# A hybrid decoder step on one core: an earlier first step of the output projection, later gate products, and interleaved norm chains at the end

## The chip, the cores and the metric

The kernel runs on one core of one Trainium2 chip. Its time is the device time of one execution in microseconds (us); smaller is better. Times in the kernel's course are counted from the start of the profiled span.

## What is computed

One inference step of a one-layer decoder. A prompt of 1024 rows and 8 decode rows (1032 rows of width 2048) pass one input projection; an attention group with sparse top-k keys and an mLSTM group work on its parts; both results are multiplied by gates, sent through one output projection, added to the input and normalised.

```python
def merge(x, att_o, p, h_ml, ml_norm_w, w_out):
    B, T, _ = x.shape
    a = att_o.astype(x.dtype) * jax.nn.silu(p['az'])
    hn = h_ml * lax.rsqrt(jnp.mean(h_ml * h_ml, axis=-1, keepdims=True) + RMS_EPS)
    hn = hn * ml_norm_w.astype(jnp.float32).reshape(ML_HEADS, ML_V_DIM)
    mo = hn.reshape(B, T, ML_WIDTH).astype(x.dtype) * jax.nn.sigmoid(p['mo']) * jax.nn.silu(p['mz'])
    return x + jnp.concatenate([a, mo], axis=-1) @ w_out
...
    y_prompt = rmsnorm(xp, final_norm_w)
```

The change concerns only `merge`, its gates `az`, `mo`, `mz` (the last columns of the input projection), and the final `rmsnorm`.

## The kernel before

Every float32 operand of a matmul is split into a high part H and a low part L, and a product is three matmuls: H by H, H by L, L by H. The split of a 128x512 weight block is one cast on ACT (`wH`) and one subtraction on DVE (`wL`). Instructions of an engine run in the order in which they stand; `pin` and the `Ordered` wrappers (`oV`, `oS`, `oG`, `oY`, `oP`) keep hand-written parts in program order, and the rest is placed by a scheduler.

**The end of the input projection.** Gate columns are made by the loop over `seq` (L1890 on) with a Strassen-like scheme of seven products of 12 matmuls each, named by their operand: ..., S4, S3, A22. S3 and A22 of the last pair accumulate in the same PSUM bank `A_`: DVE must read `A_` after S3 (`out(v, 1, 2, A_, sv[1])`, L1758) before A22 goes on in it, and read it again after A22 (`out(v, 0, 2, A_, eng=V)`, L1760). Where another pair follows, its first product `w0` stands between S3 and A22; for the last pair there is none. What A22 gives becomes the last gate: ACT takes a tanh (L1823), DVE multiplies (L1824), and a DMA of the POOL queue stores it in `gateS` (L1825).

**The last 264 rows.** Rows 768 to 1031 go through the output projection first (`rest_step`, from `seq2`): a step is 12 matmuls of 128x264 with one weight block, already split by `cut_early` (steps one to six) or `cut2` (from step seven on). The other operand is made of "mixes", one per 128 features: a gate is loaded back from `gateS` (POOL queue, L1424), multiplied with the attention or mLSTM rows (`mx`, L1436 or L1438), and split into `mH` (ACT, L1441) and `mL` (DVE, L1442). The mixes numbered 6 and 7 are the last; they need the last gate. ACT's order has their two casts ahead of the weight cast of step seven (`wraw`).

**The first 768 rows.** Four turns c = 0 to 3 of seven products each (`prods`, j = 1 to 7: A11, A12, S1, S2, S4, S3, A22) give the rows in 6 blocks of 128 and 4 column groups of 512 (`yt[b][g]`). A product is 4 blocks k, each 9 matmuls of 128x512; while PE works on block k of one product, `cut3` splits block k of the next one, and `some(2)` runs two closures of the list `filler`. `begin()`, called after j = 3 of the first turn, loads attention rows (`mo`) and gates (`gx`) for the second half of the features and puts eight gate products (`one(n)`, on DVE) into `filler`.

**The end.** The last product (c = 3, j = 7) runs row block by row block. For each of the blocks b = 3, 4, 5: `evict` adds PSUM to `yt[b][1]` (DVE), `done` squares it with a row sum (ACT), `row_scale` makes the mean and the -0.5 power (two DVE operations, POOL), and `scale1`/`scale2` scale four tiles (two on ACT, two on DVE), each stored at once by SP (`put`). Column group 3 of these blocks was multiplied by the norm weight on POOL before. Blocks 0 to 2 are done the same way shortly ahead of that, as closures of `filler`.

Of the kernel before, what the change touches and what calls it, by code (L numbers as in the profile page):

```python
# [8 lines left out]
F32 = mybir.dt.float32  # L9
# [150 lines left out]
def body(tc, A, stop=None):  # L160
# [1729 lines left out]
    for v, (ph, n) in enumerate(seq):  # L1890
# [103 lines left out]
        product(w1, A_, "A22", False, True)
        with hi():
            out(v, 0, 2, A_, eng=V)
            if w0:
                seed(v + 1, A_, B_)
            if move:
                f2 = fill_load("A22", nx)  # L2000
                fill(f1)
                k = (turn[0] + 1) % 8
                free.extend(stage[k:] + stage[:k])
                for _ in range(4):
                    pfetch()
                fill(f2)
# [5 lines left out]
        now += 4  # L2012
    flush()

    korder = PRE
    oV, oS, oG, oY, oP = (Ordered(x, pin) for x in (V, SC, G, SY, PE))
    ready2 = ready + early_w
    ready.clear()
    c0, cn = CB[0]
    held = {}  # L2020

    def flat(x):
        return x.rearrange("p a b -> p (a b)")

    def split2(src, pool, bufs):
        H, L = [pool.tile([128, 4, 128], F32R, name="w" + x, bufs=bufs) for x in "HL"]
        oS.copy(H, src)
        oV.tensor_tensor(L, src, H.bitcast(F32), OP.subtract)
        return H, L

    def rest_step(t, q, H, L):
        if t not in held:
            held[t] = bank()[:, :cn]
        for k in range(4):
            mH, mL = mixb[0][korder[q * 4 + k]]
            for z, (w_, x_) in enumerate(((H, mH), (H, mL), (L, mH))):
                oP.matmul(held[t], w_[:, k, :], x_, start=(q + k + z == 0), stop=(q == 3 and k == 3 and z == 2))

    n1 = len(ready2)
    while mids and mids[0][1] not in PRE[12:]:  # L2040
        mixmake(*mids.pop(0))
    cut = {}

    def cut_early(j):
        cut[j] = split2(ready2[j], wst, 3)
# [235 lines left out]
    def row_scale(bs, last):
        b0, b1 = bs[0], bs[-1] + 1
        oV.tensor_scalar(ss[:, b0:b1, 5], ss[:, b0:b1, last], 1.0 / D, None, OP.mult)
        oV.tensor_tensor(ss[:, b0:b1, 5], ss[:, b0:b1, 5], ss[:, b0:b1, 4], OP.add)
        oG.tensor_tensor(ss[:, b0:b1, 6], ss[:, b0:b1, 5], mhalf.to_broadcast([128, b1 - b0]), OP.pow)

    def put(q, b, g):
        q.dma_start(A["yP"][b, :, g * 512:g * 512 + 512], yt[b][g])

    def scale1(b, last):  # L2290
        r, y = ss[:, b, 6:7], yt[b]
        u = min(g for g in range(4) if g != last)
        oS.activation(y[u], y[u], AF.Copy, scale=r)
        put(oY, b, u)
        oV.scalar_tensor_tensor(y[last], y[last], r, fw[last], OP.mult, OP.mult)
        put(oY, b, last)

    def scale2(b, last):
        r, y = ss[:, b, 6:7], yt[b]
        _, v, w = (g for g in range(4) if g != last)  # L2300
        oS.activation(y[v], y[v], AF.Copy, scale=r)
        put(oY, b, v)
        oV.tensor_scalar(y[w], y[w], r, None, OP.mult)
        put(oY, b, w)

    def done(bs, g):
        last = 3 if bs[0] < 3 else 1
        for b in bs:
            jk = pf[0].tile([128, 512], BF16, name="jk", bufs=2)
            oS.activation(jk, yt[b][g], AF.Square, accum_out=ss[:, b, g:g + 1])  # L2310
            if g != last:
                oG.tensor_tensor(yt[b][g], yt[b][g], fw[g], OP.mult)
        b0, b1 = bs[0], bs[-1] + 1
        if g == (1 if last == 3 else 3):
# [5 lines left out]
                oV.tensor_scalar(ss[:, b0:b1, 4], ss[:, b0:b1, 4], 1.0 / D, EPS, OP.mult, OP.add)  # L2320
            filler.append(sums)
        if g == last == 3:
            filler.extend((lambda: None, lambda: None, lambda: row_scale(bs, last), lambda: None, lambda: None))
            filler.extend(lambda b=b, f=f: f(b, last) for b in bs for f in (scale1, scale2))
        elif g == last:
            row_scale(bs, last)
            for b in bs:
                scale1(b, last)
                scale2(b, last)

    def gather1(b, g, p, sign):
        if (b, g) not in seen:
# [47 lines left out]
    def begin():  # L2380
# [105 lines left out]
    for p, d in enumerate(prods):  # L2486
        c, j = d["c"], d["j"]
        if p == len(prods) - 1:
            some(99)
            for b in range(3):  # L2490
                for k in range(4):
                    block(p, b, k, *cuts[p * 4 + k])
                evict(p, (b,))
                after(p, (b,))
            break
        for k in range(4):
            H, L = cuts.pop(p * 4 + k)
# [104 lines left out]
```

## Time and profile before

| | |
|---|---|
| median of 3 runs | 2017.35 us (2016.02 to 2018.61) |
| the profiled execution | 2015.65 us |
| its span in the profile | 2013.9 us |
| PE busy in the span | 1959.7 us |
| mean granted TensorE clock | 0.992 |

The profile is of one execution; 1.75 us of its time lie outside the span. A row of the timeline reads: start, duration, engine, line, operation, output and inputs, shapes, count, and in brackets the idle time of the engine before it with what ended it. L157 is the line of the `Ordered` helper, so that most instructions of the output projection bear it. Consecutive operations of DVE and ACT overlap by about 0.1 us, so that the distance of two starts is shorter than a duration.

### The profile page before, as it was taken

To read this page: it belongs to the slowest core of one execution; us is meant where nothing else is said; L and a number is where in the kernel's file an instruction comes from. 1 tells how busy PE (TensorE), PEld (TensorE's weight loads), DVE (VectorE), ACT (ScalarE), POOL (GpSimd) and SP (SyncE) were. 2 spreads that over 40 slices of the span, in tenths; PEclk is the share of its full clock that TensorE was granted. 3 is DMA by queue.
4 is the path that set the end of the run, shared out by engine and by line. 5 is a ranking of instruction groups with operands and counts; after the bars stand their busy time and mean duration, and the time that the engine had idled before them with its cause. 6 is when DMAs were issued, how large, how long until landed. Compare 5 with 4: busy or idle time off the path is not lost.

```text
span 2013.9 us, 35597 instructions
## 1 busy us (share of the span) xinstructions
PE 1959.7 (97%) x12404; PEld 1867.9 (93%) x12404; DVE 1310.4 (65%) x3115; ACT 1020.8 (51%) x2183; POOL 333.6 (17%) x442
## 2 busy tenths in 40 slices
PE   9999999999999999999999999989999999999997
PEld 8999999999999999998999999989999989978785
DVE  8574465446555563884667677677777677856766
ACT  8243246653343878313556565645555445535544
POOL 0000101100000000043000000132322230224472
PEclk9999999999999999999999999999999999999998
DMA  7686654532222222278456777499887868899994
GB/s 245 196 271 189 211 180 140 166 110 79 74 68 64 65 71 63 75 237 230 110 141 187 208 191 192 133 296 282 249 254 221 235 195 268 272 263 202 210 212 151
DMA packets 259821, 362.80 MB, mean 180 GB/s; under 512 B 39109, under 2 KB 156937, under 8 KB 259641
## 3 DMA queue, kind: packets, MB, share of 16 engines
q1 hardware_dynamic: 231945, 301.48, 48.3%
q0 software_dynamic: 27264, 58.87, 14.7%
q8 instruction: 97, 1.59, 0.3%
q14 instruction: 83, 0.68, 0.1%
q10 hardware_dynamic: 432, 0.18, 0.0%
HBM read 274.19 MB, written 86.23 MB: 179 GB/s over the span
## 4 chain that ended last, share of the span: by engine, by line
PE 60%; DMA 7%; DVE 6%; ACT 3%; issue 3%; POOL 1%; SPq 0%; ACTq 0%; DVEq 0%; POOLq 0%
PE pj L1459 20%; PE pj L1705 16%; PE bank L157 8%; PE pj L157 5%; PE bank L629 2%; PE bank L680 2%; DMA xP<-in_wa_dram 2%; PE bank L478 2%; PE bank L671 1%; PE bank L1459 1%; ACT gt L523 1%; DMA qkv<-mlS 1%; DVE wL L157 1%; PE bank L1705 1%; DVE wL L1695 1%
## 5 line engine op out<-in xcount | busy, mean ns | idle before, releaser
L1459 PE MATMUL pj<-xQ,wH 128*128 128x388 f32 (+1 forms) x1808 | 473.4, 340 | 3.9 <-ACT ev L371 2.9
L1705 PE MATMUL pj<-xQ,wH 128*128 128x388 f32 x1248 | 332.5, 344 | 6.4 <-DVE pj L1830 2.4
L1459 PEld LDWEIGHTS pj<-xQ,wH 128*128 128x128 f32 (+1 forms) x1808 | 321.8, 187 | 7.6 <-ACT ev L371 3.9
L1459 PE MATMUL pj<-xQ,wL 128*128 128x388 f32 (+1 forms) x904 | 307.2, 340 | 0.0
L1705 PEld LDWEIGHTS pj<-xQ,wH 128*128 128x128 f32 x1248 | 223.6, 189 | 9.8 <-DVE pj L1830 3.5
L1705 PE MATMUL pj<-xQ,wL 128*128 128x388 f32 x624 | 214.2, 343 | 1.1 <-DVE wL L1695 1.1
L235 ACT CAST wH<-wraw 128x512 fp32r<-128x512 f32 (+3 forms) x151 | 90.8, 604 | 223.2 <-PE pj L1459 186.3
L1459 PE MATMUL pj<-xP,wH 128*128 128x256 f32 (+1 forms) x896 | 172.5, 284 | 2.4 <-ACT ev L371 1.8
L236 DVE TENSOR_TENSOR wL<-wraw,wH 128x512 fp32r<-128x512 f32 (+3 forms) x151 | 101.2, 674 | 109.2 <-ACT wH L235 108.2
L1459 PEld LDWEIGHTS pj<-xQ,wL 128*128 128x128 f32 (+1 forms) x904 | 169.0, 187 | 1.8 <-issue 0.7
L157 DVE TENSOR_TENSOR wL<-wb,wH 128x512 fp32r<-128x512 f32 x150 | 117.1, 787 | 73.4 <-ACT wH L157 59.1
L1705 PE MATMUL pj<-xP,wH 128*128 128x256 f32 x768 | 147.8, 285 | 0.9 <-ACT ev L1745 0.9
L1459 PEld LDWEIGHTS pj<-xP,wH 128*128 128x128 f32 (+1 forms) x896 | 143.6, 187 | 4.7 <-ACT ev L371 2.3
L1695 DVE TENSOR_TENSOR wL<-xP,wH 128x512 fp32r<-128x512 f32 x168 | 115.6, 689 | 49.5 <-ACT wH L1694 47.3
L157 ACT CAST wH<-wb 128x512 fp32r<-128x512 f32 x150 | 91.7, 619 | 109.3 <-PE pj L157 53.3
L1694 ACT CAST wH<-xP 128x512 fp32r<-128x512 f32 x168 | 103.6, 618 | 82.2 <-PE pj L1705 68.8
L1459 PE MATMUL pj<-xP,wL 128*128 128x256 f32 (+1 forms) x448 | 126.2, 282 | 0.0
L1705 PEld LDWEIGHTS pj<-xP,wH 128*128 128x128 f32 x768 | 122.3, 189 | 1.8 <-ACT ev L1745 1.2
L480 ACT ACTIVATE rl<-bank 128x512 f32<-128x512 f32 (+2 forms) x160 | 79.5, 523 | 83.7 <-PE bank L478 59.7
L1705 PEld LDWEIGHTS pj<-xQ,wL 128*128 128x128 f32 x624 | 118.0, 189 | 2.0 <-DVE wL L1695 1.4
L483 DVE SCALAR_TENSOR_TENSOR s<-rl,wiN,s 128x512 f32<-128x512 f32 (+2 forms) x150 | 94.9, 657 | 30.4 <-ACT rl L480 27.3
L1705 PE MATMUL pj<-xP,wL 128*128 128x256 f32 x384 | 108.9, 284 | 0.0
(517 smaller groups left out, 4580.5 us busy)
## 6 DMA issues: line engine op xcount, KB each, us to landing
wraw<-in_wa_dram SPq DMA_DIRECT2D x166, 256.0 KB
xP<-in_wa_dram SPq DMA_DIRECT2D x120, 256.0 KB
wb<-in_wt_dram SPq DMA_DIRECT2D x64, 256.0 KB
wb<-in_wt_dram POOLq DMA_DIRECT2D x64, 256.0 KB
wb<-in_wo_dram SPq DMA_DIRECT2D x38, 256.0 KB
part<-ev SPq DMA_DIRECT2D x48, 194.0 KB
xR<-part SPq DMA_DIRECT2D x47, 194.0 KB
y<-in_xT_dram SPq DMA_DIRECT2D x16, 516.0 KB
```

The source lines that it names most:

```text
L157: return lambda *a, **k: self.pin(f(*a, **k))
L235: a = SC.copy(H[:, s, :cols], raw[:, s, :cols])
L236: return a, V.tensor_tensor(L[:, s, :cols], raw[:, s, :cols], H[:, s, :cols].bitcast(F32), OP.subtract)
L478: PE.matmul(p[:, :cn], qi[:, h % 4, :], ki[x][:, c0:c0 + cn], start=(x == 0), stop=(x == 1))
L480: SC.activation(r[:, :cn], p[:, :cn], AF.Relu)
L483: v = V.scalar_tensor_tensor(s[:, c0:c0 + cn], r[:, :cn], wv, s[:, c0:c0 + cn], OP.mult, OP.add)
L629: PE.matmul(p[:, :cn], a_[:, h, :], b_[:, c0:c0 + cn], start=(z == 0), stop=(z == 2))
L680: PE.matmul(oT[:, :256], a_[:, k2 + kk, :], b_[:, ks_], start=(k2 + kk == 0 and z == 0), stop=(k2 + kk == i and z == 2))
L1459: m = PE.matmul(ps[:cols, :cn], w_[:, k, :cols], xv(kk, xz, c0, cn), start=(n0 == 0 and k == 0 and z == 0), stop=(n0 == n9 and k == 3 and ...
L1694: SC.copy(H, src)
L1695: V.tensor_tensor(L, src, H.bitcast(F32), OP.subtract)
L1705: PE.matmul(ps[:, :n], w_[:, k, :], REG[reg][k](xz), start=(first and k == 0 and z == 0), stop=(last and k == 3 and z == 2), skip_group_ch ...
```

## The change

Three edits. First, for the last pair of `seq`, step one of `rest_step` stands between S3 and A22, and the weight splits of steps one to three are issued there (`cut_early` and its helpers move up for that). Second, `begin()` puts eight empty closures ahead of the eight gate products. Third, the chains at the end are rewritten: blocks 0 to 2 take their scale at once instead of through `filler`, the chains of blocks 3 to 5 are written interleaved, the POOL products with the norm weight for column group 3 of these blocks are gone (DVE's `scaled_w` multiplies by scale and weight in one operation instead), and mean plus constant is one operation.

```diff
             w1 = split(T4, v)
+            if not w0:
+                cut_early(0)
+                cut_early(1)
         if w0:
             product(w0, B_, "A11", True, True)
+        else:
+            rest_step(*seq2[0], *cut.pop(0))
         product(w1, A_, "A22", False, True)
         with hi():
             out(v, 0, 2, A_, eng=V)
             if w0:
                 seed(v + 1, A_, B_)
+            else:
+                cut_early(2)
...
-    for j in range(3):
-        cut_early(j)
-    for i in range(3):
+    cut_early(3)
+    for i in range(1, 3):
         rest_step(*seq2[i], *cut.pop(i))
         cut_early(i + 3)
...
+    def row_scale(b, last):
+        oV.scalar_tensor_tensor(ss[:, b, 5:6], ss[:, b, last:last + 1], 1.0 / D, ss[:, b, 4:5], OP.mult, OP.add)
+        oG.tensor_tensor(ss[:, b, 6:7], ss[:, b, 5:6], mhalf, OP.pow)
+
+    def put(b, g):
+        oY.dma_start(A["yP"][b, :, g * 512:g * 512 + 512], yt[b][g])
+
+    def scaled(b, g):
+        oS.activation(yt[b][g], yt[b][g], AF.Copy, scale=ss[:, b, 6:7])
+        put(b, g)
+
+    def scaled_w(b, g):
+        oV.scalar_tensor_tensor(yt[b][g], yt[b][g], ss[:, b, 6:7], fw[g], OP.mult, OP.mult)
+        put(b, g)
...
-            if g != last:
+            square(b, g)
+            if g != last and (b < 3 or g != 3):
                 oG.tensor_tensor(yt[b][g], yt[b][g], fw[g], OP.mult)
...
         if g == last == 3:
-            filler.extend((lambda: None, lambda: None, lambda: row_scale(bs, last), lambda: None, lambda: None))
-            filler.extend(lambda b=b, f=f: f(b, last) for b in bs for f in (scale1, scale2))
...
+            for b in bs:
+                row_scale(b, 3)
+            for b in bs:
+                filler.append(lambda b=b: (scaled(b, 0), scaled_w(b, 3)))
+                filler.append(lambda b=b: (scaled(b, 1), scaled_v(b, 2)))
...
+        filler.extend([lambda: None] * 8)
         filler.extend(lambda n=n: one(n) for n in range(8))
...
                 evict(p, (b,))
-                after(p, (b,))
+                square(3 + b, 1)
+
+            first(0)
+            row_scale(3, 1)
+            evict(p, (1,))
+            scaled(3, 0)
+            scaled_w(3, 1)
+            square(4, 1)
+            scaled_w(3, 3)
+            scaled(3, 2)
+            row_scale(4, 1)
+            evict(p, (2,))
...
```

The order of the instructions, at three places. First ACT's at the end of the input projection, before; the `ev` row is the last gate, `mH` rows are the casts of mixes (19269 and 19273 are mixes 6 and 7), the first `wraw` row and the `xP` rows cast the weight blocks of steps one to six, and the last row those of steps seven and eight:

```order
L1441 CAST mH_19050<-mx 128x264
L1441 CAST mH_19161<-mx 128x264
L1441 CAST mH_19165<-mx 128x264
L1823 ACTIVATE ev<-xR_14875 128x388
L157 CAST wH<-wraw 128x512 x2
L157 CAST wH<-xP_9730 128x512 x2
L157 CAST wH<-xP_9731 128x512 x2
L1441 CAST mH_19269<-mx 128x264
L1441 CAST mH_19273<-mx 128x264
L157 CAST wH<-wraw 128x512 x2
```

The same stretch of ACT now (mixes 6 and 7 are 19294 and 19298); the casts of steps one and two stand some rows ahead of it:

```order
L157 CAST wH<-xP_9730 128x512
L1441 CAST mH_19050<-mx 128x264
L1441 CAST mH_19161<-mx 128x264
L1823 ACTIVATE ev<-xR_14875 128x388
L157 CAST wH<-xP_9730 128x512
L157 CAST wH<-xP_9731 128x512
L1441 CAST mH_19165<-mx 128x264
L157 CAST wH<-xP_9731 128x512
L1441 CAST mH_19294<-mx 128x264
L1441 CAST mH_19298<-mx 128x264
L157 CAST wH<-wraw 128x512 x2
```

The weight casts of steps one to three moved ahead of the last gate; those of steps seven and eight stay behind mixes 6 and 7. On PE the 12 matmuls of step one now stand ahead of the 12 of A22.

Second, DVE's order in the first turn, before; `wL` rows are weight splits (`wb_19395` to `wb_19398` are the four blocks of product j = 5, `wb_19391` to `wb_19394` those of j = 6), `mo<-gx` rows are the gate products:

```order
L157 TENSOR_TENSOR wL<-wb_19395,wH 128x512
L157 SCALAR_TENSOR_TENSOR mo_21022<-gx,mo_21022 128x384
L157 SCALAR_TENSOR_TENSOR mo_21024<-gx,mo_21024 128x384
L157 TENSOR_TENSOR wL<-wb_19396,wH 128x512
L157 SCALAR_TENSOR_TENSOR mo_21026<-gx,mo_21026 128x384
L157 SCALAR_TENSOR_TENSOR mo_21028<-gx,mo_21028 128x384
L157 TENSOR_TENSOR wL<-wb_19397,wH 128x512
```

And now:

```order
L157 TENSOR_TENSOR wL<-wb_19395,wH 128x512
L157 TENSOR_TENSOR wL<-wb_19396,wH 128x512
L157 TENSOR_TENSOR wL<-wb_19397,wH 128x512
L157 TENSOR_TENSOR wL<-wb_19398,wH 128x512
L157 TENSOR_TENSOR wL<-wb_19391,wH 128x512
L157 TENSOR_TENSOR wL<-wb_19392,wH 128x512
L157 SCALAR_TENSOR_TENSOR mo_21022<-gx,mo_21022 128x384
L157 SCALAR_TENSOR_TENSOR mo_21024<-gx,mo_21024 128x384
L157 TENSOR_TENSOR wL<-wb_19393,wH 128x512
L157 SCALAR_TENSOR_TENSOR mo_21026<-gx,mo_21026 128x384
```

The first gate product moved from ahead of the second block's split of j = 5 to behind the second block's split of j = 6, five splits later.

Third, the end of DVE's order as a piece of the difference; `ss` rows are the mean, `yt` rows with `pj` the evictions of the last product's three row blocks, and those with `ss` and `fnr` the scaling:

```order
 L157 TENSOR_TENSOR yt_21246<-pj_20778,yt_21246 128x512
-L157 TENSOR_SCALAR ss<-ss 128x1
-L157 TENSOR_TENSOR ss<-ss 128x1
+L157 SCALAR_TENSOR_TENSOR ss<-ss 128x1
+L157 TENSOR_TENSOR yt_21247<-pj_20779,yt_21247 128x512
 L157 SCALAR_TENSOR_TENSOR yt_21246<-yt_21246,ss,fnr_21914 128x512
-L157 TENSOR_SCALAR yt_21252<-yt_21252,ss 128x512
-L157 TENSOR_TENSOR yt_21247<-pj_20779,yt_21247 128x512
-L157 TENSOR_SCALAR ss<-ss 128x1
-L157 TENSOR_TENSOR ss<-ss 128x1
+L157 SCALAR_TENSOR_TENSOR yt_21252<-yt_21252,ss,fnr_21918 128x512
+L157 SCALAR_TENSOR_TENSOR ss<-ss 128x1
```

The eviction of a block moved ahead of the scaling of the block before it.

More of the change, by code (lines that the diff above doesn't have):

```diff
@@ L1879, in body, with flat, split2, rest_step @@
     stage.clear()
+    korder = PRE
+    oV, oS, oG, oY, oP = (Ordered(x, pin) for x in (V, SC, G, SY, PE))
+    cn = CB[0][1]
+    held = {}
+    def flat(x):
+        return x.rearrange("p a b -> p (a b)")
+    def split2(src, pool, bufs):
+        H, L = [pool.tile([128, 4, 128], F32R, name="w" + x, bufs=bufs) for x in "HL"]
+        oS.copy(H, src)
+        oV.tensor_tensor(L, src, H.bitcast(F32), OP.subtract)
+        return H, L
+    def rest_step(t, q, H, L):
+        if t not in held:
+            held[t] = bank()[:, :cn]
+        for k in range(4):
+            mH, mL = mixb[0][korder[q * 4 + k]]
+            for z, (w_, x_) in enumerate(((H, mH), (H, mL), (L, mH))):
+                oP.matmul(held[t], w_[:, k, :], x_, start=(q + k + z == 0), stop=(q == 3 and k == 3 and z == 2))
+    cut = {}
+    def cut_early(j):
+        cut[j] = split2((ready + early_w)[j], wst, 3)
     pj = [psj.tile([128, 512], F32, name=f"pj{c}") for c in range(3)]
@@ L2013, in body @@
     flush()
-    korder = PRE
-    oV, oS, oG, oY, oP = (Ordered(x, pin) for x in (V, SC, G, SY, PE))
     ready2 = ready + early_w
-    ready.clear()
     c0, cn = CB[0]
[L2020 to L2037, printed above, removed]
     n1 = len(ready2)
@@ L2041, in body @@
         mixmake(*mids.pop(0))
-    cut = {}
-    def cut_early(j):
-        cut[j] = split2(ready2[j], wst, 3)
-    for j in range(3):
-        cut_early(j)
-    for i in range(3):
+    cut_early(3)
+    for i in range(1, 3):
         rest_step(*seq2[i], *cut.pop(i))
@@ L2279, in add_x, with scaled_v, square @@
         oG.dma_start(yt[b][g], A["x2"][b, :, g * 512:g * 512 + 512], accum_op=OP.add)
[L2281 to L2304, printed above, removed]
+    def row_scale(b, last):
[9 more added lines that the diff above has]
+        put(b, g)
+    def scaled_v(b, g):
+        oV.tensor_scalar(yt[b][g], yt[b][g], ss[:, b, 6:7], None, OP.mult)
+        put(b, g)
+    def square(b, g):
+        jk = pf[0].tile([128, 512], BF16, name="jk", bufs=2)
+        oS.activation(jk, yt[b][g], AF.Square, accum_out=ss[:, b, g:g + 1])
     def done(bs, g):
@@ L2308, in done @@
         for b in bs:
-            jk = pf[0].tile([128, 512], BF16, name="jk", bufs=2)
-            oS.activation(jk, yt[b][g], AF.Square, accum_out=ss[:, b, g:g + 1])
-            if g != last:
+            square(b, g)
+            if g != last and (b < 3 or g != 3):
                 oG.tensor_tensor(yt[b][g], yt[b][g], fw[g], OP.mult)
@@ L2322, in done @@
         if g == last == 3:
-            filler.extend((lambda: None, lambda: None, lambda: row_scale(bs, last), lambda: None, lambda: None))
-            filler.extend(lambda b=b, f=f: f(b, last) for b in bs for f in (scale1, scale2))
-        elif g == last:
-            row_scale(bs, last)
             for b in bs:
-                scale1(b, last)
-                scale2(b, last)
+                row_scale(b, 3)
+            for b in bs:
+                filler.append(lambda b=b: (scaled(b, 0), scaled_w(b, 3)))
+                filler.append(lambda b=b: (scaled(b, 1), scaled_v(b, 2)))
     def gather1(b, g, p, sign):
@@ L2492, in body, with first @@
                     block(p, b, k, *cuts[p * 4 + k])
+            def first(b):
                 evict(p, (b,))
-                after(p, (b,))
+                square(3 + b, 1)
[9 more added lines that the diff above has]
+            evict(p, (2,))
+            scaled_w(4, 1)
+            scaled(4, 0)
+            square(5, 1)
+            row_scale(5, 1)
+            scaled_w(4, 3)
+            scaled(4, 2)
+            scaled_w(5, 1)
+            scaled(5, 0)
+            scaled_w(5, 3)
+            scaled(5, 2)
             break
```

## The prediction

> **What bounds the kernel now.** I read the page's totals first, then who waits for whom on PE over the whole span, then the timeline at the longest waits, and last the windows for the granted clock. The totals, and the four waits of PE at the places that the change touches (total, times, longest):
>
> ```profile
> PE 1959.7 (97%) x12404; PEld 1867.9 (93%) x12404; DVE 1310.4 (65%) x3115; ACT 1020.8 (51%) x2183; POOL 333.6 (17%) x442
> ```
>
> ```profile
> PE pj L157 <- DVE wL L157: 3.1, 1, 3.1
> PE bank L157 <- DVE wL L157: 2.0, 6, 0.7
> PE bank L157 <- issue: 1.8, 1, 1.8
> PE pj L1705 <- DVE xR L1758: 0.9, 1, 0.9
> ```
>
> PE bounds the kernel: 1959.7 us busy of a span of 2013.9, and no matmul is removed. So the change can win only at PE's waits, at the clock, and behind PE's last matmul. The clock makes waits dear. A wait at 100 us, and then windows: length, busy time of PE, PEld, DVE, ACT and POOL with counts, granted clock, DMA share, GB/s.
>
> ```profile
> 100.55 0.62 PE L1459 MATMUL bank<-xQ,wH 128*128 128x388 f32 x2 [1.66 <-ACT wH L235]
> ```
>
> ```profile
> 102.00:103.00 1.00, 1.00 (x5) 1.00 (x5) 1.00 (x3) 0.74 (x3) 0.00 (x0) 0.50 0.63 152
> 1654.90:1658.30 3.40, 1.43 (x8) 0.93 (x7) 3.13 (x8) 2.49 (x5) 0.85 (x2) 1.00 0.24 87
> 1658.30:1661.70 3.40, 3.40 (x18) 3.40 (x17) 1.37 (x3) 0.62 (x1) 1.07 (x2) 0.50 0.76 240
> 1798.25:1801.65 3.40, 2.80 (x7) 2.22 (x8) 2.70 (x5) 0.00 (x0) 0.00 (x0) 0.50 1.07 384
> 1801.65:1805.05 3.40, 3.40 (x10) 2.63 (x9) 3.23 (x6) 0.62 (x1) 0.00 (x0) 0.50 1.04 374
> ```
>
> After a stretch with PE busy for 1.43 us of 3.40 the clock is 0.50 for the next 3.4 us, though PE works all through it: 1.7 us lost. Behind the 3.1 us wait it is 0.50 for 6.8 us; in the first half PE was busy for 2.80 of 3.40, too little to end it. At 100 us one wait of 1.66 us was enough. I take from this that a wait of some 1.7 us or more costs itself and then 1.7 to 3.2 us of clock, by where it falls on a grid of 3.4 us.
>
> [...]
>
> **First edit: step one ahead of A22.** PE's starts of A22 and of steps one, five and seven of the last 264 rows; then the last gate's product, the load of mixes 6 and 7, mix 7's cast, step seven's weight split, and the next weight loads.
>
> ```profile
> 1653.03 0.59 PE L1705 MATMUL pj<-xQ,wH 128*128 128x388 f32 x2 [0.94 <-DVE xR L1758]
> 1657.15 0.36 PE L157 MATMUL bank<-mH,wH 128*128 128x264 f32 x1 [1.77 <-issue]
> 1665.06 0.28 PE L157 MATMUL bank<-mH,wH 128*128 128x264 f32 x1
> 1667.99 0.28 PE L157 MATMUL bank<-mH,wH 128*128 128x264 f32 x1
> 1656.57 0.56 DVE L1824 SCALAR_TENSOR_TENSOR ev<-ev,xR 128x388 f32<-128x388 f32 x1 [0.25 <-ACT ev L1823]
> 1660.05 1.07 POOL L1424 DMA_DIRECT2D mL<-gateS x2 [2.07 <-DMA gateS<-ev]
> 1665.74 0.41 ACT L1441 CAST mH<-mx 128x264 fp32r<-128x264 f32 x1 [1.14 <-DVE mx L1436]
> 1666.33 1.14 ACT L157 CAST wH<-wraw 128x512 fp32r<-128x512 f32 x2 [0.18 <-ACT mH L1441]
> 1666.99 1.29 DVE L157 TENSOR_TENSOR wL<-wraw,wH 128x512 fp32r<-128x512 f32 x2 [0.37 <-ACT wH L157]
> 1665.04 1.75 SPq L157 DMA_DIRECT2D wb<-in_wo_dram  x4
> ```
>
> A step takes 1.46 us (1665.06 to 1667.99 is two). I take step one's operands as ready by then, since its splits now stand well ahead, so it fills the 0.94 us wait while DVE reads the bank, and the splits of steps two and three no longer stand behind the last gate. S3 ends at 1653.03 - 0.94 = 1652.1, and A22 takes 1657.15 - 1.77 - 1653.03 = 2.35; with step one, A22 and steps two to six back to back PE is through six steps at 1652.1 + 6 x 1.46 + 2.35 = 1663.2, where before it was at 1667.99: 4.8 us ahead.
>
> Most of that is given back at step seven. Its weight cast stands on ACT behind mix 7, and mixes 6 and 7 wait for the last gate's way through memory. That chain doesn't start earlier: the gate's product now has a weight split (0.6) and two mix operations (0.35 each) ahead of it on DVE where before there was one mix operation, so it comes about 0.9 us later. Against that, mix 6 and mix 7 are no longer interrupted by the splits of steps five and six (1 us). I put step seven's cast at 1665.9 to 1666.6, PE's start at 1666.5 to 1667: 1.0 us ahead is what is left. The new wait of 3.3 to 3.8 us then brings the half clock, 1.7 to 3.2 us; I take 2.1, since a single stretch is the commoner case. The next weight loads (1665.04) wait for the slots of step six and go out over 4 us sooner, so the later small waits (the other five of the 2.0 us, 1.8 us) should go. Sum: 1.0 + 1.8 - 2.1 = 0.7 us gained. Ends: 2.5 us lost (two half-clock stretches, 0.7 us ahead, no small wait gone), 3.8 gained (no half clock, 2.0 ahead, all small waits gone).
>
> **Second edit: gate products later.** PE's starts of products j = 4, j = 5, of the second block of j = 5 after its wait, and of j = 6; then DVE's first gate products and the weight split behind them.
>
> ```profile
> 1784.82 0.62 PE L157 MATMUL bank<-wH,rS 128*128 128x512 f32 x2
> 1793.06 0.62 PE L157 MATMUL pj<-wH,rS 128*128 128x512 f32 x2
> 1798.85 0.80 PE L157 MATMUL pj<-wL,rS 128*128 128x512 f32 x1 [3.12 <-DVE wL L157]
> 1807.54 0.62 PE L157 MATMUL bank<-wH,rS 128*128 128x512 f32 x2
> 1795.51 0.56 DVE L157 SCALAR_TENSOR_TENSOR mo<-gx,mo 128x384 f32<-128x384 f32 x1 [7.33 <-DMA mo<-attS]
> 1797.64 0.56 DVE L157 SCALAR_TENSOR_TENSOR mo<-gx,mo 128x384 f32<-128x384 f32 x1 [1.57 <-DMA gx<-gateS]
> 1798.11 0.69 DVE L157 TENSOR_TENSOR wL<-wb,wH 128x512 fp32r<-128x512 f32 x1
> ```
>
> DVE waited 7.3 us for the first rows and 1.6 for the next gate; the split of block two, behind both, came at 1798.11. A product takes 1793.06 - 1784.82 = 8.24 us; this one took 14.48. The 6.24 us over are 3.12 of wait and 3.12 of half clock. Now five more splits stand ahead of the first gate product. Each frees a weight buffer only when PE is done with a block, so DVE gets to it at about 1798.6, when both loads have landed, and PE needs nothing behind it before 1803.4, the second block of j = 6. What is late next is nothing within 3 us. I take 6.2 us; ends 3.1 (the wait alone) and 6.2.
>
> **Third edit: the end.** POOL's weight products, one of DVE's operations beside them, the evictions of the three blocks, PE's last matmul, block 3's square, the last two scalings on ACT, the 24 stores of SP (shortest, median, longest issue, then first and last start), and two windows at the end.
>
> ```profile
> 1991.25 4.42 POOL L157 TENSOR_TENSOR yt<-yt,fnr 128x512 f32<-128x512 f32 x3 [3.03 <-ACT jk L157]
> 1993.01 1.51 DVE L157 TENSOR_SCALAR yt<-yt,ss 128x512 f32<-128x512 f32 x1
> 1998.14 0.68 DVE L157 TENSOR_TENSOR yt<-pj,yt 128x512 f32<-128x512 f32 x1
> 2001.74 0.68 DVE L157 TENSOR_TENSOR yt<-pj,yt 128x512 f32<-128x512 f32 x1
> 2005.35 0.68 DVE L157 TENSOR_TENSOR yt<-pj,yt 128x512 f32<-128x512 f32 x1
> 1998.85 0.39 PE L157 MATMUL pj<-wL,rA 128*128 128x512 f32 x1
> 1998.91 0.63 ACT L157 ACTIVATE jk<-yt 128x512 bf16<-128x512 f32 x1 [3.44 <-DVE yt L157]
> 2007.88 1.33 ACT L157 ACTIVATE yt<-yt,ss 128x512 f32<-128x512 f32 x2 [1.03 <-POOL ss L157]
> ```
>
> ```profile
> L157 SPq DMA_DIRECT2D out_yP_dram<-yt x24: 332/389/593, 1989.0 to 2010.0; - x24
> ```
>
> ```profile
> 2011.00:2012.00 1.00, 0.00 (x0) 0.00 (x0) 0.00 (x0) 0.00 (x0) 0.00 (x0) 0.50 1.03 389
> 2012.00:2013.00 1.00, 0.00 (x0) 0.00 (x0) 0.00 (x0) 0.00 (x0) 0.00 (x0) 0.50 0.23 84
> ```
>
> PE is done with block 5 at 1998.85 + 0.39 = 1999.2 and with blocks 4 and 3 a third of a product (8.24 / 3) earlier each, at 1996.5 and 1993.7; DVE evicts them at 1998.14, 2001.74 and 2005.35. The first is late because DVE still scales blocks 0 to 2, slowed by POOL; the others because each chain (3.6 us: evict, square, power, scale) is run to its end first. Now blocks 0 to 2 are scaled one product earlier, POOL's 4.42 us are gone, and each eviction stands ahead of the scaling of the block before. I followed the new order row by row with the durations above: evictions at 1993.9, 1996.5 and 1999.3, where PE sets them; then the last square, power and two scalings beside block 4's, at an end of 2003.1 instead of 2009.2. The one fused mean operation saves nothing that counts; the three `scaled_w` in place of plain scalings cost 0.3 us each, included. The stores become the limit: the last issue moves from 2010.0 to 2004.1, but 8 stores of 256 KB now start from 2000.7 on, and at 389 GB/s they take 5.4 us, from 2001.7 to 2007.1, where the last bytes landed at 2012.2 before. So 5.1 us, not 6.1; ends 2.5 (stores spaced as now, chains overlapping only in part) and 6.1.
>
> **Sum.** 0.7 + 6.2 + 5.1 = 12.0 us off the profiled execution's 2015.65 us: 2003.7. The median of before lies 1.7 us above that execution, and in others the 3.1 us wait can cost 1.6 instead of 3.1 us of clock, which makes 2017.35 - 10.5 = 2006.8 from there. I forecast 2004.5, between the two and nearer to the traced one. What a measurement of this kernel can tell from no change is about 0.2%, 4 us.
>
> **The rivals.** One (0.15): the first edit loses. The clock falls for two stretches at step seven and the later waits stay: 0.7 becomes -2.5, 2007.7. For it: the wait spans more than a window; against it: only one of the drops above lasted twice.
> Two (0.08): the gate loads are still late at the new place, PE waits again, half as long, and the clock falls: 3.1 of the 6.2 stay, 2007.6. For it: landings at 1795.5 and 1797.6 leave about 1 us; against it: DVE's lateness is covered by 4 us.
> Three (0.04): the half clock doesn't come from the waits but from elsewhere, and stays: 3.1 less, 2007.6. Against it stand the rows at 100, 1658 and 1798 us.
> Four (0.08): the stores bind harder, 2.5 instead of 5.1: 2007.1.
> Five, slower (0.03): SP's queue. The loads of the last eight gates now stand behind five more weight loads, the last of which wait for splits of j = 6. DVE first needs them here:
>
> ```profile
> 1839.84 1.02 DVE L157 SCALAR_TENSOR_TENSOR mo<-yt,mo 128x384 f32<-128x384 f32 x2
> ```
>
> That is 1833.6 in the new time, and I expect them issued by 1816. Each us of landing past 1833.6 costs PE one; past 1846 the whole gain is gone, and 10 us later still the time would be 2025. Nothing in the trace points there.
>
> **Chances.** The forecast has 0.62. Its own terms and rivals one to four all stay faster; only several together come within 4 us of before. Faster 0.92, same 0.05, slower 0.03. The range goes down to 2000.0 (first and third edit at their best, 3.1 + 1.0 more) and up to 2009.5 (one rival, and another in part).
>
> **What the new profile would show.** First edit: no wait before A22; ACT's cast of step seven at about its old distance to the last gate; a PE wait of 3 to 4 us ahead of step seven and a 0.50 clock behind it. Second: j = 5 in 8.2 us, no DVE wait for `gx` or `mo` that PE feels, clock 1.00. Third: evictions 2.6 to 2.9 us apart, PE's end to the span's end about 9.5 us instead of 2013.9 - 1999.2 = 14.7, DMA share near 1 in the last 5 us. The prediction is wrong if j = 5 is still above 10 us, if step seven starts later than before, or if the end keeps more than 12 us behind PE.

## The result, and the profile after

The changed kernel takes 2001.3 us (median of 7 runs, 1998.4 to 2004.2) where the kernel before took 2017.35 us in the same series (2009.3 to 2020.7). The ratio is 0.9937, with a 95% interval of 0.992 to 0.9955: faster by 0.63%, about 13 us, where 12.8 were forecast. The two medians alone lie 16 us apart, at the far end of that interval. On the chips of the later runs the kernel before had a median of 2012 us, and the changed kernel, run again there, gave 0.9946 (0.9927 to 0.9966), 11 us. The profiled execution of the changed kernel took 1999.92 us, with a span of 1998.1.

The totals of the changed kernel's profile, and its waits of PE at the places of the change (total, times, longest):

```profile
PE 1953.5 (98%) x12404; PEld 1863.1 (93%) x12404; DVE 1307.1 (65%) x3113; ACT 1021.3 (51%) x2183; POOL 342.9 (17%) x441
```

```profile
PE bank L157 <- ACT wH L157: 3.8, 1, 3.8
PE bank L157 <- DVE wL L157: 0.2, 1, 0.2
```

The 3.1 us wait of `pj` for `wL`, the 1.8 us wait before step one and the 0.9 us wait before A22 are gone, five of the six small waits too, and one wait of 3.8 us is new. Three rows of PE cut the span into pieces: S3's last matmul, the first 128x512 matmul (the first 768 rows begin), and the last matmul. The profile gives the span to 0.1 us, so the piece behind the last matmul is good to some 0.05 us. Before (the row of its last matmul stands in the prediction) and after:

```profile
1651.75 0.33 PE L1705 MATMUL pj<-xQ,wL 128*128 128x388 f32 x1
1756.95 0.64 PE L157 MATMUL bank<-wH,rA 128*128 128x512 f32 x2
```

```profile
1649.40 0.34 PE L1705 MATMUL pj<-xQ,wL 128*128 128x388 f32 x1
1752.05 0.64 PE L157 MATMUL bank<-wH,rA 128*128 128x512 f32 x2
1988.35 0.40 PE L157 MATMUL pj<-wL,rA 128*128 128x512 f32 x1
```

| piece | before | after | gained | forecast |
|---|---|---|---|---|
| up to S3's last matmul | 1651.75 | 1649.40 | 2.35 | 0 |
| from there to the first 128x512 matmul (first edit) | 105.20 | 102.65 | 2.55 | 0.7 |
| from there to PE's end (second edit) | 242.29 | 236.70 | 5.59 | 6.2 |
| from PE's end to the span's end (third edit) | 14.66 | 9.35 | 5.31 | 5.1 |

**First edit.** The way to step seven in the changed kernel: the last gate's product, the load of mixes 6 and 7, mix 6, mix 7's cast, step seven's weight cast, PE's step seven; then two windows of the clock.

```profile
1655.14 0.55 DVE L1824 SCALAR_TENSOR_TENSOR ev<-ev,xR 128x388 f32<-128x388 f32 x1
1658.43 1.08 POOL L1424 DMA_DIRECT2D mL<-gateS  x2 [1.90 <-DMA gateS<-ev]
1661.59 0.43 DVE L1436 SCALAR_TENSOR_TENSOR mx<-mL,mH 128x264 f32<-128x264 f32 x1 [3.75 <-DMA mL<-gateS]
1663.32 0.41 ACT L1441 CAST mH<-mx 128x264 fp32r<-128x264 f32 x1 [0.84 <-DVE mx L1436]
1663.91 1.14 ACT L157 CAST wH<-wraw 128x512 fp32r<-128x512 f32 x2 [0.18 <-DMA wb<-in_wo_dram]
1664.58 0.59 PE L157 MATMUL bank<-mH,wH 128*128 128x264 f32 x1 [3.83 <-ACT wH L157]
```

```profile
1661.00:1664.40 3.40, 0.00 (x0) 0.00 (x0) 1.65 (x4) 1.31 (x3) 0.00 (x0) 1.00 1.02 360
1664.40:1667.80 3.40, 3.22 (x13) 3.00 (x14) 3.24 (x6) 2.78 (x7) 0.00 (x0) 0.50 0.75 262
```

The weight cast of step seven stands behind mix 7, whose gate comes through memory; PE is idle for 3.83 us, and the next 3.4 us run at half clock.

**Second edit.** Starts of products j = 5 and j = 6, and DVE's first gate products, with no idle time ahead of them:

```profile
1788.19 0.62 PE L157 MATMUL pj<-wH,rS 128*128 128x512 f32 x2
1796.43 0.62 PE L157 MATMUL bank<-wH,rS 128*128 128x512 f32 x2
1793.56 1.02 DVE L157 SCALAR_TENSOR_TENSOR mo<-gx,mo 128x384 f32<-128x384 f32 x2
```

j = 5 takes 8.24 us (1796.43 - 1788.19), as j = 4 did before (1793.06 - 1784.82). PE does not wait once between 1771.6 and 1863.5.

**Third edit.** The three evictions, the last scalings, SP's stores, and the DMA engines at the end:

```profile
1983.18 0.69 DVE L157 TENSOR_TENSOR yt<-pj,yt 128x512 f32<-128x512 f32 x1 [0.73 <-PE pj L157]
1985.98 0.69 DVE L157 TENSOR_TENSOR yt<-pj,yt 128x512 f32<-128x512 f32 x1 [1.10 <-PE pj L157]
1988.78 0.69 DVE L157 TENSOR_TENSOR yt<-pj,yt 128x512 f32<-128x512 f32 x1 [0.72 <-PE pj L157]
1991.58 1.33 ACT L157 ACTIVATE yt<-yt,ss 128x512 f32<-128x512 f32 x2 [0.68 <-POOL ss L157]
```

```profile
L157 SPq DMA_DIRECT2D out_yP_dram<-yt x24: 332/432/599, 1974.8 to 1994.0; - x24
```

```profile
1995.00:1996.00 1.00, 0.00 (x0) 0.00 (x0) 0.00 (x0) 0.00 (x0) 0.00 (x0) 0.50 1.05 385
1996.00:1997.00 1.00, 0.00 (x0) 0.00 (x0) 0.00 (x0) 0.00 (x0) 0.00 (x0) 0.50 0.51 188
```

Each eviction now waits for PE, not for DVE. After the last scaling (1993) only stores are left, and they keep the DMA engines full to 1996.5. There is one cost that was not forecast: the scalings of blocks 0 to 2 stand ahead of j = 6's evictions on DVE, and PE waits 0.54 us before the last product's first block (e9 and e10, where these scalings run later, don't have this wait):

```profile
1980.11 0.47 PE L157 MATMUL pj<-wH,rA 128*128 128x512 f32 x1 [0.54 <-issue]
```

### The profile page after: what moved, and what is told of

It is laid out like the page before. It is cut to its first block, busy times and chain, and to the rows that moved or that the text cites. A ratio compares the mean times of both kernels' runs of the same rounds, so it can differ in the third digit from the quotient of the medians.

```text
span 1998.1 us, 35595 instructions
## 1 busy us (share of the span) xinstructions
PE 1953.5 (98%) x12404; PEld 1863.1 (93%) x12404; DVE 1307.1 (65%) x3113; ACT 1021.3 (51%) x2183; POOL 342.9 (17%) x441
## 4 chain that ended last, share of the span: by engine, by line
PE 59%; DMA 7%; DVE 7%; issue 3%; ACT 3%; POOL 1%; SPq 0%; DVEq 0%; POOLq 0%; ACTq 0%
PE pj L1459 17%; PE pj L1705 16%; PE bank L157 9%; PE pj L157 5%; PE bank L629 2%; PE bank L680 2%; DMA xP<-in_wa_dram 2%; PE bank L478 2%; PE bank L671 1%; ACT gt L523 1%; DMA qkv<-mlS 1%; PE bank L1705 1%; DVE jk L1295 1%; DVE wL L1695 1%; DMA xP<-sS 1%
```

## The experiments

The profiles of all runs, cut at the same three rows of PE (us):

| run | S3's last to first 128x512 | to PE's end | PE's end to span's end |
|---|---|---|---|
| before | 105.20 | 242.29 | 14.66 |
| changed | 102.65 | 236.70 | 9.35 |
| e1, first edit alone | 104.55 | 238.87 | 14.67 |
| e2, second edit alone | 104.30 | 236.00 | 14.51 |
| e3, third edit alone | 105.75 | 241.61 | 9.38 |
| e4, splits ahead of the mixes | 102.90 | 236.70 | 9.40 |
| e5, e4 with loads later | 105.99 | 236.72 | 9.37 |
| e6, two empty closures | 103.60 | 237.45 | 9.38 |
| e7, POOL's products kept | 104.09 | 236.87 | 10.32 |
| e8, chains in turn | 103.38 | 236.72 | 10.17 |
| e9, scaling begun late | 104.06 | 235.94 | 11.44 |
| e10, e4 joined with two edits | 101.27 | 242.21 | 9.42 |
| e11, e10 with mixes later | 100.17 | 242.76 | 9.37 |
| e12, changed again | 103.47 | 236.68 | 9.45 |

### e1: the first edit alone

```diff
+            if not w0:
+                cut_early(0)
+                cut_early(1)
...
+        else:
+            rest_step(*seq2[0], *cut.pop(0))
...
+            else:
+                cut_early(2)
...
```

> The first edit alone on the kernel before. Theory: the waits before A22 and step one (0.94, 1.77, 0.20 us) go, a wait of 3.3 to 3.9 us stands before step seven with one stretch of half clock behind it, the small waits of the later steps go; from S3's last matmul to the first 128x512 matmul of the output projection 2.0 to 2.8 us less than before (105.2), the whole run 0.5 to 3 us less than before. Rival one of the prediction: 2.5 us longer. A second rival, from the changed kernel's profile: the earlier splits make the matmul at the L1830 seed wait for a late gate load (2.95 us against 0.86); then that wait is near 3 us here too and takes the gain away; by the theory it is chance, and is 0.2 to 1.5 us here.

Measured: 0.9995 of the time before (0.9982 to 1.0008), no difference that can be told from zero. The piece takes 104.55 us, which lies among those of the three profiles without the edit (105.20, 104.30, 105.75). The wait before step seven was 4.59 us, longer than expected, and the half clock lasted two stretches (6.8 us), with PE busy for 2.52 us of the 3.41 of the first. So rival one of the prediction came halfway: the clock fell for two stretches, but the small waits went, and the edit was still not slower. The wait at L1830 was 0.98 us, against the second rival; e3, without the edit, had 1.93.

The unexpected thing is j = 5, which this kernel leaves as it was. PE's wait there, and the windows around it:

```profile
1799.57 0.50 PE L157 MATMUL pj<-wL,rS 128*128 128x512 f32 x1 [2.39 <-DVE wL L157]
```

```profile
1795.15:1798.56 3.41, 2.04 (x9) 1.32 (x8) 0.76 (x2) 1.29 (x3) 0.00 (x0) 1.00 0.88 264
1798.56:1801.97 3.41, 2.40 (x10) 1.86 (x11) 2.97 (x6) 0.62 (x1) 0.00 (x0) 1.00 1.05 383
1668.87:1672.28 3.41, 2.52 (x10) 2.29 (x11) 2.97 (x6) 2.82 (x7) 0.00 (x0) 0.51 0.69 218
```

A wait of 2.39 us cost no clock at all. The windows are laid on the grid that this run's own drop shows (it began at 1668.87; 38 times 3.413 later is 1798.56; all spells of the profile of before start at multiples of 3.413 us from each other, last section): the wait lies across a border, and PE is busy for about 60% of the first window and for 70% of the second. The third row is the first of the two half-clock stretches behind step seven: with PE busy for 2.52 of 3.41 us the half clock went on for a second one. This kernel is not alone in that. Behind step seven the half clock lasted 6.8 us in e7, e8 and e9 as well, and 3.4 us in the changed kernel, e6 and e12; the two stretches of e9:

```profile
1667.84:1671.25 3.41, 1.25 (x4) 1.03 (x5) 2.15 (x6) 2.34 (x5) 0.00 (x0) 0.50 0.84 300
1671.25:1674.66 3.41, 3.41 (x18) 3.41 (x17) 3.41 (x8) 1.90 (x4) 0.00 (x0) 0.50 0.81 229
```

### e2: the second edit alone

```diff
+        filler.extend([lambda: None] * 8)
         filler.extend(lambda n=n: one(n) for n in range(8))
```

> The second edit alone on the kernel before. Theory: product j = 5 of the first turn takes 8.2 us instead of 14.5, half of the gain by the wait and half by the clock, so 5.6 to 6.2 us off the time, clock 1.00 through that product. Rival (the half clock has another cause than the wait): the clock still falls to 0.50 there, 3.1 us off.

Measured: 0.9975 (0.9959 to 0.999), 5 us. In the profile the piece is 6.29 us shorter than before (242.29 to 236.00), with no wait and a clock of 1.00 through j = 5. The rival is out: with the wait the half clock went too. What the edit is worth changes with the execution, since the half clock that it saves does: 6.3 us against the profile of before, 2.9 against that of e1 (238.87).

### e3: the third edit alone

```diff
-            filler.extend(lambda b=b, f=f: f(b, last) for b in bs for f in (scale1, scale2))
+            for b in bs:
+                row_scale(b, 3)
...
+            evict(p, (1,))
+            scaled(3, 0)
...
```

> The third edit alone on the kernel before. Theory: from PE's last matmul to the span's end 9.3 to 9.8 us instead of 15.1, evictions 2.7 to 2.9 us apart, 5 us off the time. Rival (stores bind): 12 us or more from PE's end, 2.5 us off.

Measured: 0.9976 (0.9965 to 0.9986), 4.8 us; the end takes 9.38 us instead of 14.66, and the wait of 0.53 us before the last product is here too, so that 5.28 - 0.53 = 4.75 is what the edit gives. The times of the three edits alone add up to 0.05 + 0.25 + 0.24 = 0.54%, what the whole change gave in e12 (0.9946). The wait in j = 5 was 3.06 us here, and the half clock lasted one stretch, not two:

```profile
1793.63:1797.04 3.41, 0.75 (x3) 0.67 (x4) 1.63 (x3) 0.00 (x0) 0.00 (x0) 1.00 1.02 347
1797.04:1800.45 3.41, 3.41 (x9) 2.61 (x9) 2.77 (x6) 0.62 (x1) 0.00 (x0) 0.51 1.05 382
1800.45:1803.86 3.41, 3.41 (x16) 2.82 (x15) 3.41 (x8) 0.82 (x2) 0.00 (x0) 0.99 1.02 368
```

### e4: the splits of steps seven to nine ahead of the last mixes

```diff
...
+    for j in (6, 7, 8):
+        ahead[j] = wst.tile([128, 4, 128], F32, name="wraw", bufs=2)
+        oY.dma_start(ahead[j], A["wo"][seq2[j]])
+        rest_step(*seq2[j - 3], *cut.pop(j - 3))
+        cut[j] = split2(ahead[j], wst, 3)
     while mids:
         mixmake(*mids.pop(0))
...
```

> The changed kernel, with the weight splits of steps seven and eight put ahead of mixes 6 and 7 on ACT and DVE, that of step nine between them. Theory (step seven waits for its place in ACT's order, not for data): the 3.83 us wait goes; what is left is at most 2 us in front of step nine or ten, which needs the mixes of the last gate; no half clock; from S3's last matmul to the first 128x512 matmul 2.5 to 5 us less than the changed kernel's 102.65, and as much off the time. Rival (data bind: the weights' loads or the mixes): a wait of 3 us or more moves to step seven, eight or ten, the clock falls again, and nothing is gained.

Measured: 0.9949 (0.9932 to 0.9967), not faster than the changed kernel; the piece takes 102.90 us, 0.25 more. The theory was right about step seven and wrong about the end. Step seven started 4.0 us sooner (11.21 us after S3's last matmul instead of 15.18), step eight 5.6 us sooner, with no half clock. But the next wait came at step nine:

```profile
1667.91 0.39 PE L157 MATMUL bank<-mH,wH 128*128 128x264 f32 x1 [1.82 <-ACT wH L157]
```

```profile
1667.24 0.62 ACT L157 CAST wH<-wraw 128x512 fp32r<-128x512 f32 x1 [2.47 <-DMA wraw<-in_wo_dram]
```

ACT waited for step nine's raw weights. Of the 5.6 us, 1.9 were lost at step nine, and all of the rest at small waits up to step 28. So the rival's outcome came (nothing is gained) without the wait of 3 us that it named.

### e5: e4 with the mixes' loads later

```diff
-    next(mixes)
...
-        if i > 3:
-            next(mixes, None)
+        if i > 11:
+            next(mixes, None)
+        if i in (11, 24, 28, 32, 36, 40, 44, 48, 52):
+            next(mixes, None)
```

> The kernel of run e4_split_ahead, with the loads of the first products' mixes (mo and mg, 192 KB each) begun eight steps later. Theory (in e4 the steps behind nine wait for their raw weights, since 0.8 MB of mo and mg stand among them on SP's queue and the DMA engines are full): the waits of 0.57, 0.48, 0.38 and 0.39 us behind step nine shrink to less than 0.5 together, and from S3's last matmul to the first 128x512 matmul it is 100.3 to 101.8 us instead of 102.9; 1 to 2.5 us off the time of e4. Rival (the splits on ACT and DVE bind, or PE waits later for the mixes): 102.5 or more, or the first products wait longer by as much.

Measured: 0.9958 (0.9943 to 0.9972); the piece takes 105.99 us, 3 us longer than in e4, as the rival had it. Yet the reason held as far as it went: from step 11 to step 28, PE no longer waited, and was 3.55 us ahead of e4 at step 28. From there on the catching up (two mix operations instead of one between two splits) made DVE late for PE; the longest of seven waits:

```profile
1745.79 0.39 PE L157 MATMUL bank<-mH,wL 128*128 128x264 f32 x1 [1.17 <-DVE wL L157]
```

By the last step the 3.55 us had become 3.09 behind.

### e6: two empty closures instead of eight

```diff
-        filler.extend([lambda: None] * 8)
+        filler.extend([lambda: None] * 2)
```

> The changed kernel with two empty closures instead of eight ahead of the gate products, so that the first of them stand behind the split of the second block of j = 5, ahead of that of the third. Theory: the loads land when they did, PE has one block (2.06 us) more to do before it must wait, so a wait of 0.8 to 1.6 us in j = 5 instead of 3.12, and no half clock, since a wait of that length leaves every stretch of 3.4 us more than half busy; 1 to 2 us slower than the changed kernel. By the prediction's rule (from 1.7 us on a wait costs clock) the same; if any idle time were enough, 1.7 to 3 us more.

Measured: 0.9959 (0.9942 to 0.9976). The wait in j = 5 is 0.37 us, shorter than expected, with the clock at 1.00 in it, and the piece is 0.75 us longer than in the changed kernel:

```profile
1802.55 0.50 PE L157 MATMUL pj<-wL,rS 128*128 128x512 f32 x1 [0.37 <-DVE wL L157]
```

One block's delay is nearly enough; the other four blocks are reserve.

### e7, e8, e9: the third edit in parts

e7 keeps POOL's products, e8 runs the chains one after the other, e9 scales blocks 0 to 2 as late as before:

```diff
-            if g != last and (b < 3 or g != 3):
+            if g != last:
...
```

```diff
...
+            for b in range(3):
+                evict(p, (b,))
+                square(3 + b, 1)
+                row_scale(3 + b, 1)
+                scaled(3 + b, 0)
+                scaled_w(3 + b, 1)
+                scaled(3 + b, 2)
+                scaled_w(3 + b, 3)
```

```diff
-            for b in bs:
-                row_scale(b, 3)
+            filler.extend((lambda: None, lambda: None))
+            filler.append(lambda: [row_scale(b, 3) for b in bs])
+            filler.extend((lambda: None, lambda: None))
```

> The changed kernel with POOL's three 128x512 products with the norm weight kept (DVE then scales these tiles plainly). Theory: the interleaving and the earlier scaling carry most of the third edit; POOL's 4.42 us beside DVE delay block 3's eviction by 0.5 to 1.5 us, from PE's last matmul to the span's end 9.4 to 11 us (9.35 in the changed kernel, 14.66 before). Rival (POOL's products were what made the end late): over 12 us.

> The changed kernel with the chains of blocks 3, 4 and 5 run one after the other, without POOL's products. Theory: each chain takes 3.6 us against 2.75 us between the blocks, so that the last eviction is 1.7 to 2.5 us later than in the changed kernel and the tail 10.5 to 12 us (9.35 in the changed kernel). Rival (the stores bind, not the chains): 9.3 to 9.8 us, as the DMA engines have only 3 MB to move.

> The changed kernel with the scaling of blocks 0 to 2 begun as late as before: two empty closures, the three means, two empty closures, then the scalings, all through filler. Theory (of what is left of the 5.3 us after runs e7 and e8, which lost 0.97 and 0.82, the earlier scaling carries most): DVE still scales blocks 0 to 2 after j = 6's evictions, block 3's eviction comes 1 to 2.5 us later than PE ends it, and the tail is 10.5 to 12.5 us instead of 9.35. Rival (the interleaving, the missing POOL products and the earlier scaling each cover for the others): under 10 us. The wait of 0.53 us before the last product's first block should go, since the evictions stand ahead of three scalings again.

Measured: 0.9954 (0.9935 to 0.9972), 0.9945 (0.9924 to 0.9966) and 0.9942 (0.9921 to 0.9962): the times can't tell costs of 1 or 2 us, the profiles can. The end takes 0.97, 0.82 and 2.09 us more than in the changed kernel. POOL's products, two of DVE's small sums beside them and the first eviction in e7; the second and the third eviction in e8; the first eviction in e9:

```profile
1979.77 4.24 POOL L157 TENSOR_TENSOR yt<-yt,fnr 128x512 f32<-128x512 f32 x3 [6.28 <-ACT jk L157]
1981.54 2.50 DVE L157 TENSOR_TENSOR ss<-ss 128x3 f32<-128x3 f32 x2
1984.15 0.68 DVE L157 TENSOR_TENSOR yt<-pj,yt 128x512 f32<-128x512 f32 x1
```

```profile
1988.06 0.68 DVE L157 TENSOR_TENSOR yt<-pj,yt 128x512 f32<-128x512 f32 x1
1991.74 0.69 DVE L157 TENSOR_TENSOR yt<-pj,yt 128x512 f32<-128x512 f32 x1
```

```profile
1989.85 0.68 DVE L157 TENSOR_TENSOR yt<-pj,yt 128x512 f32<-128x512 f32 x1
```

Two sums of 128x3 elements, 0.16 us each in the changed kernel, take 2.50 us beside POOL. Counted from PE's end, the first eviction stands 5.6 us ahead in the changed kernel, 3.6 in e7 (1987.78 - 1984.15; 2.0 us later, where 0.5 to 1.5 were expected), 4.1 in e9 (1993.96 - 1989.85) and 1.1 before. In e8 the evictions are 3.7 us apart and the last comes 1.8 us after PE's end; the end is only 0.8 us longer (10.17, under the 10.5 expected), as in the changed kernel the stores are behind at the last, and here they had time to catch up (DMA share 0.33 from 1995 to 1996, 1.04 in the two us behind it). So e8's rival holds in part, those of e7 and e9 are out, and in e9 the 0.53 us wait of PE is gone, as expected. Of the 5.3 us these three account for 3.9; the rest lies in how they cover for each other or in the mean's shorter form, which was not tried alone.

### e10, e11 and e12: can more be had?

e10 joins e4 with a later start of the mixes, without catching up, and moves the last two scalings of blocks 0 to 2 behind j = 6's evictions. e11 also makes the mixes one turn later in the input projection. e12 is the changed kernel again, on the same chip.

```diff
...
-        if i > 3:
+        if i > 10:
             next(mixes, None)
...
-                some(3 if c == 0 and j < 4 else 2)
+                some(3 if c == 0 and j < 4 else 0 if c == 3 and j == 6 and k == 2 else 2)
```

```diff
-        if len(mids) > 3 or mids and not pend:
+        if len(mids) > 5 or mids and not pend:
```

> The kernel of run e4_split_ahead with two more edits: the first products' mixes begin seven steps later without being caught up (what is left of them runs when the steps are through), and the last two scalings of blocks 0 to 2 run after j = 6's evictions. Theory: from S3's last matmul to the first 128x512 matmul 98.5 to 100.5 us (102.65 in the changed kernel), since the weights' loads no longer wait and DVE is not crowded by catching up; the wait of 0.53 us before the last product goes; 2.5 to 4.5 us faster than the changed kernel. Rival: the mixes left over hold up the first products (a wait in j = 1 or j = 2 of 2 us or more) and nothing is gained.

> The kernel of run e10_joined, with the mixes of the last 264 rows made one turn later in the input projection (from six waiting loads on, not four). Theory (the wait at L1830, 0.4 to 2.95 us in the profiles so far, is DVE held by a mix whose gate load is late): that wait falls under 0.3 us, with no half clock around 1620; 1 to 4 us faster than e10, and a narrower spread of the times. Rival: the mixes then crowd the last pairs, and PE waits for them at A22 or at step one.

> The changed kernel once more, on the chip of runs e9 to e11, to compare them with it: 0.9937 of the time before (0.992 to 0.9955) by the first measurement; the wait at L1830 anywhere between 0.4 and 3 us, the wait before step seven 3.8 to 4.6 us, the tail 9.3 to 9.4 us.

Measured: e10 0.9958 (0.9944 to 0.9973), e11 0.9942 (0.9923 to 0.996), e12 0.9946 (0.9927 to 0.9966). e10 is faster than the changed kernel up to the first 128x512 matmul (101.27, short of the 98.5 to 100.5 expected; 2.2 us less than e12), and loses more than that 16 us later, as its rival said, though at another engine. A wait of PE, and POOL's rows behind it:

```profile
1765.53 0.58 PE L157 MATMUL bank<-cst,rr 128*128 128x128 f32 x3 [4.45 <-POOL rr L157]
```

```profile
1759.49 0.88 POOL L157 DMA_DIRECT2D wb<-in_wt_dram  x1 [5.02 <-DMA wb<-in_wt_dram]
1764.28 1.20 POOL L157 TENSOR_TENSOR rr<-rr,mhalf 128x3 f32<-128x3 f32 x1
```

The -0.5 power of the last rows' norm stands on POOL behind weight loads of the same queue, which now wait 5 us for an earlier load. With the half clock (0.50 from 1766.1 to 1769.5) that is 6.3 us lost (242.21 against 235.94 in e9, where the 0.53 us wait is gone as well). e11 brings the piece to 100.17, but keeps 3.83 us of the wait for POOL. It has no wait at L1830, but neither have e4, e5, e10 and e12, so that its theory stays open. In e12 the wait before step seven (4.20 us) and the end were as expected; the wait at L1830 was expected and did not come. No version that is measurably faster than the changed kernel was found; e11 with that power ahead of POOL's loads is the next to try, and was not tried.

## Why the prediction was right

The time (2001.3 for 2004.5), the sign and the range held, and so did each edit's mechanism; for the first edit the profiles show it, while its worth alone can't be told from zero in the times (e1). Two things in the working did not hold: the size of the small waits, and the rule for the clock. By its steps:

- **PE through six steps, and step seven.** Right to 0.3 us. S3 came 2.35 us earlier in the changed kernel's execution; with that added, step six ended at 1663.1 (1663.2 said), ACT cast step seven's weights at 1666.3 (1665.9 to 1666.6), and PE started at 1666.9 (1666.5 to 1667). The new wait was 3.83 us (3.3 to 3.8) and one stretch of half clock cost 1.65 us (2.1 taken). That it was a single stretch was luck: at this place two stretches came in four of the seven profiles with this edit and step seven as written (e1, e7, e8, e9), so the reason given, that a single one is the commoner case, does not hold here.
- **The small waits behind it** were mis-sized: 1.8 us said, 3.1 found (2.55 less the 1.06 by which step seven came sooner, plus the 1.65 of half clock), since each cost more than its idle time. Before, step ten to step eleven took 2.47 us instead of 1.46 with one wait of 0.73, and steps 16 to 20 took 7.59 instead of 5.86 with waits of 0.21, 0.22 and 0.48: about 0.27 us more for each wait. This is most of the difference between 0.7 and 2.55. Over all profiles the edit is worth less: seven with it and step seven as written average 103.7, three without it 105.1, so 1.4 us.
- **The second edit** was right in mechanism, and its range (3.1 to 6.2) holds what was found to 0.1 us: 5.59 in the changed kernel (6.13 without the 0.54 us wait that the third edit puts into this piece), 6.29 in e2, 5 us timed. That the half clock belongs to the wait is shown by e2. The rule used for it, that a wait of 1.7 us or more costs clock, is wrong: 2.39 us cost none in e1, nor did 1.82 in e4. In these profiles it went with where the wait fell: the two windows across which the 2.39 us lay had PE busy for 2.04 and 2.40 of 3.41 us, the one ahead of the fall at 1658.3 before for 1.43 (last section).
- **The third edit.** With the 10.5 us that PE's end came earlier added, the evictions were at 1993.7, 1996.5 and 1999.3, where 1993.9, 1996.5 and 1999.3 were said; the last compute at 2003.5 (2003.1), the last bytes at 2007.0 (2007.1). The stores do bind the last 3 us, as the sum had it. Missed was the 0.54 us wait that the earlier scalings put before the last product.
- **The 2.35 us ahead of S3** belong to no edit: the matmuls up to there are the same. The two executions lose clock at different places; the changed one lost 2.95 us and a stretch of half clock (0.50 from 1616.6 to 1620.0) at L1830, where DVE stood with a mix that waited for a gate load:

```profile
1615.05 0.49 DVE L1438 SCALAR_TENSOR_TENSOR mx<-mH,nw,mL 128x264 f32<-128x264 f32 x1 [4.00 <-DMA mL<-gateS]
1616.08 0.62 PE L1705 MATMUL pj<-xQ,wH 128*128 128x388 f32 x2 [2.95 <-DVE pj L1830]
```

In the other profiles this wait was between none and 2.54 us, with the first edit (0.98, 2.54, 2.34, 0.79, 1.02, and none in e4, e5, e10 and e12) and without it (0.86, 0.41, 1.93). It can be part of why executions of one kernel spread by 10 us; no run shows how much.

- **What was luck.** The profiled execution beat its own sum by 3.8 us (1999.92 for 2003.7), and 2.35 of these are the piece ahead of S3. The forecast started from a median of 2017.35 us; on the later chips the kernel before had 2012, the gain was 11 us, and the changed kernel's median of 1999.1 us (e12) lies under the range. So the gain was forecast well, and that the time itself was met hangs on the series in which it was measured. What the three edits gave one by one (1.4 us over all profiles, 5 us timed, 4.75 us) adds up to 11.2 us, where the sum had 12.0. The lower end of the range, 4.1 us under the forecast, is 2000.4 and not 2000.0.
- **Rivals.** One came true as far as the clock goes (two stretches) in four profiles, at a lower price, since the small waits did go; two, three and five did not; four's mechanism is there (e8), at the price already in the sum.

## What to carry to other kernels

Follow the chain behind a removed wait to the next thing that is late, and price that, as with step seven: of the 5 us ahead at step six 1 was left at step seven, and e4 shows the same game going on behind it (weights, then DVE, then POOL's queue). The wait in j = 5 was worth twice its length before (3.12 us of wait and 3.12 of half clock), and one of 2.39 us there in e1 brought no half clock, so count such a wait by the execution and not once for all. To undo parts of a change of 1 to 2 us each, read pieces of the profile between fixed rows; the times of this kernel, which spread by 10 us, can't tell them.

## What was not expected of the hardware

**The clock's grid.** The half clock lasted 3.41 us or twice that in all of its 54 spells before PE's last matmul in the 14 profiles (43 single, 11 double), and its start against the wait differed from run to run. Within a profile the starts lie on one grid: the five spells of the profile of before start at 101.80, 1132.63, 1337.43, 1658.28 and 1798.23, one after the other 302, 60, 94 and 41 times 3.413 us apart, to within 0.1 us. Windows of 3.41 us that end where a spell starts show when it fell: with PE busy for 1.43 us of 3.40 (before, ahead of 1658.3), 0.75 (e3) or 0 (changed) it fell at the window's end; with 2.04 and 2.40 (e1) it did not, though the wait of 2.39 us was longer than the 1.77 at 1657. It came back at the end of a window with 3.22 (changed) or 3.41 us busy, and not with 2.52 (e1) or 2.78 (before, j = 5). With this grid laid over the whole of each profile up to PE's last matmul, the border is soft. Of the windows at full clock, all 48 in which PE was busy for less than 47% brought the fall and none with more than 65% did; of the 72 between, 6 did (in the profile of before these counts are 4 windows, and 1 of 4 between; in that of the changed kernel 3, and none of 6). The two ends of this band, a window with 1.63 us busy in e5 that did not bring it and one with 2.20 in e6 that did, each with the window behind it:

```profile
1326.70:1330.11 3.41, 1.63 (x14) 1.42 (x12) 1.38 (x3) 1.74 (x5) 0.06 (x1) 1.00 0.98 307
1330.12:1333.53 3.41, 1.17 (x5) 0.85 (x6) 3.41 (x7) 2.10 (x5) 1.98 (x3) 1.00 0.97 285
915.64:919.05 3.41, 2.20 (x14) 1.67 (x14) 2.41 (x9) 1.83 (x4) 2.80 (x4) 1.00 0.83 225
919.06:922.47 3.41, 3.41 (x15) 3.41 (x14) 1.73 (x7) 1.03 (x2) 2.81 (x4) 0.50 0.94 252
```

So the busy share alone did not decide inside the band, and what else does is not shown. From the half clock it came back after every window that was busy for more than 88%, and after none under 86%. Windows that were 22% (0.75 us of 3.41, e3) and 42% busy (1.43 of 3.40, before) were enough for the fall.

**What a wait costs.** In the profile of before a short wait of PE on a weight split cost about 0.27 us beyond the idle time that the profile shows, by the step times above; step ten to step eleven gives 0.28 in e2 and in e3 too, with waits of 0.85 and 1.12 us.
